# Copies of the normalised FFN input, and the split activations of the down-projection, at low SBUF offsets

## Chip, core and metric

The kernel runs on one core of one Trainium2 chip. The metric is the device time of one execution, in microseconds. Five engines work side by side and meet by semaphores: TensorE (PE; its weight loads are listed apart as PEld), VectorE (DVE), ScalarE (ACT), GpSimd (POOL) and SyncE (SP), which here only issues DMAs. SBUF is the on-chip memory that the engines read operands from: 128 partitions, and an *offset* below is the distance in KB from the start of a partition. PSUM holds what TensorE writes.

## What is computed

One trunk layer over 1024 tokens of width 1024: two groups of recurrent heads, an out-projection, and a feed-forward network with a 3x3 convolution over a grid of 16 x 64 tokens. The change touches only the last part:

```python
def _conv_ffn(h, w_up, conv_w, w_down, rows, cols):
    u = _dwconv2d(h @ w_up, conv_w, rows, cols)
    a, b = jnp.split(u, 2, axis=-1)
    return (jax.nn.silu(a) * b) @ w_down
...
        xl = xl + g1 * (jnp.concatenate([ml_l, hg_l], axis=-1) @ w_out[l])
        xl = xl + g2 * _conv_ffn(_modulate(_rmsnorm(xl, norm2_w[l]), sh2, sc2), w_up[l], ffn_conv_w[l],
                                 w_down[l], rows, GRID_W)
...
    return _rmsnorm(xl, final_norm_w)
```

`w_up` is 1024 x 5632 and `w_down` 2816 x 1024, all in float32.

## The kernel before

**Products in three parts.** To keep float32 accuracy, each operand is split into a rounded part and the rest (`wh`, `wl` of a weight; `h2h`, `h2l` of the FFN input; `gh`, `gl` of the gated activations), and each product is made of three matmuls: high x high, high x low, low x high. One matmul is 128x128 stationary by 128x512 moving, and each has its own weight load.

**Up.** The normalised FFN input stands transposed in eight pairs of tiles, `h2h[k]` and `h2l[k]` (128 x 1024, 4 KB in a partition each). 44 column tiles `ct` of `w_up` come in pairs `ct = j` and `NF + j`, j from 0 to 21 (NF = 22). `split_weights` loads 512 KB into `wst` (three buffers) from SP, ACT rounds it to `wh`, POOL subtracts to `wl` (four buffers each, two for one `ct`). `up_half` then runs 24 matmuls for each half of the tokens: `w[:, ws]` is stationary, `x[k]` (a half of `h2h[k]` or `h2l[k]`) moves. So one `ct` is 48 matmuls and one j is 96. The first pair is made before the last norm is done (`early`). `conv2` reads the result from PSUM: one ACT scaling, and eight DVE instructions on one `ct`; then Silu on ACT and the gate product on POOL fill `Gt[j]`. For the last j the result is copied to `src` first.

**Down.** Two halves of the output columns, `dh` = 0 and 1. For each block `c` of 128 rows of `w_down` (22 of them) `down_ops` makes `wh`, `wl` and, from `Gt[c]`, `gh` (ACT) and `gl` (DVE; POOL for c < 3 of `dh` = 0). Here the activations are stationary (`x[:, ts_]`) and the weights move; 24 matmuls for one `c`, three in a row for each of the eight token tiles. `kind` says where `gh` and `gl` stand: 0 for the first block, which is prepared while the up-projection still runs; 1 for the other blocks; 2 for the last NL = 4 blocks of `dh` = 1, whose 96 matmuls run token tile by token tile at the very end so that the final norm can follow tile by tile.

**Between the halves** `evac` scales the eight results of `dh` = 0 from PSUM into `ytmp` (DVE), `acc` adds them to `ys` (DVE) and squares the sum (ACT); POOL multiplies by the norm weight.

**Order.** PE's order is the order of the code. The other engines' and SP's order is made by a scheduler. Each engine works strictly in its order; a tile's buffer is reused only when all its readers are done, and a pool that takes over the space of another waits for that one's readers.

**Offsets** (in KB, from the memory plan of the built program; all of these tiles span 128 partitions):

| Tile | Before |
|---|---|
| `wst`; `wh`, `wl` | 17 to 29; 29 to 45 |
| in-projection input `hh`, `hl`; out-projection input `mh`, `ml` | 45 to 125; 53 to 117 |
| `h2h[0..7]`, `h2l[0..7]` | 159 to 191, 191 to 223 |
| `Gt[0..21]` | 45 to 133 |
| `gh`, `gl` of kind 0 | 137 to 145 |
| `gh`, `gl` of kind 1 (two buffers each) | 187 to 203 |
| `wd` and `gd` (weights and activations of kind 2) | 45 to 61, and 61 to 93 |

Of the kernel before, what the change touches and what calls it, by code (L numbers as in the profile page):

```python
# [9 lines left out]
F32 = mybir.dt.float32  # L10
F32R = mybir.dt.float32r
# [6 lines left out]
P = 128  # L18
D = 1024
KD = D // P  # L20
T = 1024
# [3 lines left out]
NLT = T // P  # L25
# [5 lines left out]
NF = DFF // P  # L31
# [38 lines left out]
SLOT = (4, 6, 8)  # L70
WARM = 4
NL = 4


@with_exitstack
def kernel(ctx: ExitStack, tc: tile.TileContext, A: dict, out: bass.AP):
# [3 lines left out]
    V, S, G, PE, SY = nc.vector, nc.scalar, nc.gpsimd, nc.tensor, nc.sync  # L80

    def pool(name, bufs=1, space=None, side=None):
        kw = {}
        if space is not None:
            kw["space"] = space
        if side is not None:
            kw["side"] = side
        return tc.tile_pool(name=name, bufs=bufs, **kw)
# [7 lines left out]
    def raw(ap):  # L96
        return ap.bitcast(F32)
# [24 lines left out]
    gd = dp.tile([P, P], F32, name="gd")  # L122
# [13 lines left out]
            halves.append((wh, wl))  # L136
        return halves

    # ------------------------------------------------------------ in-projection input h
    hp_cm = pool("h", side="left")  # L140
    hp = hp_cm.__enter__()
    hh = [hp.tile([P, TA], F32R, name=f"hh{k}") for k in range(KD)]
# [349 lines left out]
    act_cm.__enter__()  # L492
    st_cm.close()

    # ------------------------------------------------------------ in-projection
    CMO = {"mq": 0, "mk": 4, "mo": 8, "hq": 12, "zf": 16, "zb": 20, "hg": 24}

    def two(pl):
# [133 lines left out]
        V.tensor_tensor(lb, lbl[:, :, 0, :], lbm, op=ALU.mult)  # L632
        V.tensor_scalar(lbm, lb, -1.0, 1.0, op0=ALU.mult, op1=ALU.add)

    # ------------------------------------------------------------ mLSTM heads
    with ExitStack() as es:
        ml = es.enter_context(pool("ml", side="left"))
        mlw = es.enter_context(pool("mlw", bufs=2, side="left"))
# [5 lines left out]

        pass

        # gates
        tasks = []
        acc = [0.0, 0.0]

# [344 lines left out]
                cur = nx  # L995

    vp_cm.__exit__(None, None, None)
    # ------------------------------------------------------------ HGRN heads
    sgp_cm = pool("sg", bufs=3, side="right")
    sgp = sgp_cm.__enter__()  # L1000
    with ExitStack() as es:
# [254 lines left out]
            if h < H - 1:  # L1256
                hs = hg_out(h, QQ, At, SS)

        # -------------------------------------------------------- out-projection, norm2
        opp_cm, opp = lefts[0]  # L1260
        mh, mlo = {}, {}

# [77 lines left out]
    h2_cm = pool("h2", side="right")  # L1340
    h2p = h2_cm.__enter__()
    h2h = [h2p.tile([P, T], F32R, name=f"h2h{k}") for k in range(KD)]
    h2l = [h2p.tile([P, T], F32R, name=f"h2l{k}") for k in range(KD)]
    with ExitStack() as es:
# [75 lines left out]
                    next(norms, None)  # L1420
            xn = out_x1(accs)

        # -------------------------------------------------------- conv FFN: up
        def up_half(pl, halves, g):
            gs = slice(g * 512, (g + 1) * 512)
            for k in range(KD):
# [28 lines left out]
        return pl_tile(name) if i % 4 < 2 else psb.tile([P, T], F32, name=name, tag="plb")  # L1455


    Gp = ctx.enter_context(pool("G", side="left"))
    Gt = [Gp.tile([P, T], F32, name=f"G{j}") for j in range(NF)]
    g2bc = Gp.tile([P, D], F32, name="g2bc")  # L1460
    with ExitStack() as es:
        fp = es.enter_context(pool("ff", bufs=2, side="left"))
# [29 lines left out]

        pst = {}

        def down_ops(c, dh, kind):
            if c % 2 == 0:
                st = wp.tile([P, 2, 512], F32, name="wst", bufs=3)
                SY.dma_start(out=st, in_=A["wdown"][dh, c // 2].rearrange("p (a b) -> p a b", a=2))
                pst["s"] = st
                if kind == 2:  # L1500
                    pst["w"] = [Gp.tile([P, 2, 512], F32R, name="wd", tag=f"G{c - NF + NL + i}") for i in range(2)]
            src = pst["s"][:, c % 2, :]
            if kind == 2:
                wh, wl = [w[:, c % 2, :] for w in pst["w"]]
                gh, gl = [Gp.tile([P, T], F32R, name="gd", tag=f"G{NL + 2 * (c - NF + NL) + i}") for i in range(2)]
            else:
                wh = wp.tile([P, 512], F32R, name="wh", bufs=4)
                wl = wp.tile([P, 512], F32R, name="wl", bufs=4)
                gp_ = dn_ if kind else Gp
                gh = gp_.tile([P, T], F32R, name="gh")  # L1510
                gl = gp_.tile([P, T], F32R, name="gl")
            S.copy(wh, src)  # L1512
            G.tensor_tensor(wl, src, raw(wh), op=ALU.subtract)  # L1513
            S.copy(gh, Gt[c])  # L1514
            (G if dh == 0 and c < 3 else V).tensor_tensor(gl, Gt[c], raw(gh), op=ALU.subtract)  # L1515
            return gh, gl, wh, wl
# [7 lines left out]
            return src  # L1524

        for j in range(NF):
            if j == NF - 1:
                pre0 = down_ops(0, 0, 0)
            pl = up_src(j, j == NF - 1)
            conv2(Gt[j], pl, lambda i: fcw[:, j, i:i + 1])  # L1530
            S.activation(Gt[j], Gt[j], AF.Silu)
            pl = up_src(NF + j, j == NF - 1)
            cb = fp.tile([P, T], F32, name="cb", tag="cb")
            conv2(cb, pl, lambda i: fcw[:, NF + j, i:i + 1])
            G.tensor_tensor(Gt[j], Gt[j], cb, op=ALU.mult)
    h2_cm.__exit__(None, None, None)

    # ------------------------------------------------------------ conv FFN: down, final norm
    dn_ = ctx.enter_context(pool("dn", bufs=2, side="right"))
    d1 = ctx.enter_context(pool("d1", bufs=1, side="right"))  # L1540
    fnw = d1.tile([P, D], F32, name="fnw")
    SY.dma_start(out=fnw, in_=A["fnw"].partition_broadcast(P))
    ms_cm = tc.manual_schedule(engines={mybir.EngineType.PE})
    ms_cm.__enter__()
    ys = [d1.tile([P, D], F32, name=f"y{t}") for t in range(NLT)]
    s0 = d1.tile([P, NLT, 2], F32, name="s0")
    pre = [pre0]
    for dh in range(2):
# [19 lines left out]
                mm(t, c, *ops)  # L1568
        rest = [part(c, True) for c in range(n, NF)]

        def evac(t):
            tmp = dn_.tile([P, 512], F32, name="ytmp", bufs=8)
            V.tensor_tensor(tmp, po[t], g2bc[:, ds_], op=ALU.mult)
            return tmp

# [7 lines left out]
        if dh == 0:  # L1583
# [3 lines left out]
            for t, tmp in zip(order, tmps):  # L1587
                y = acc(t, tmp)
# [107 lines left out]
```

## Time and profile before

| | us |
|---|---|
| three runs | 1602.72, 1602.76, 1604.93; median 1602.76 |
| span of the profiled execution, first to last instruction (no other time of it is given) | 1603.1 |
| up-projection on PE | 833 to 1332 |
| down-projection, `dh` = 0, then `dh` = 1 | 1332 to 1464, to 1595 |
| last norm and stores | to 1603.1 |
| busy: PE, DVE, ACT, POOL | 1520.5, 1137.0, 551.4, 638.8 |

A matmul's row gives its start and a modelled end: matmuls overlap, so the duration (0.39 us) is longer than the distance from one start to the next. That distance, called the *step* below, is what a matmul costs in a dense row of them, and it is read from start times. In a merged row (x96) it is the row's length without one duration, over the count less one.

### The profile page before, as it was taken

What the parts mean: (1) busy time and instruction counts of PE and PEld (TensorE: products, weight loads), DVE (VectorE), ACT (ScalarE), POOL (GpSimd) and SP (SyncE); (2) the same over time, 40 slices, a digit from 0 to 9 for tenths busy, and PEclk for the clock granted to TensorE, in tenths of its full rate; (3) what the DMA queues carried; (4) which work ended last, traced back from release to release, by engine and by line L of the source; (5) the groups of instructions that cost most, each with busy time, mean ns of one, the idle gap of its engine ahead of it and who ended that gap; (6) DMA issues with size and microseconds to landing.
All of it is one profiled execution on the core that took longest, in us unless ns stands there. A gap on an engine that the chain in (4) does not pass through costs nothing.

```text
span 1603.1 us, 22297 instructions
## 1 busy us (share of the span) xinstructions
PE 1520.5 (95%) x8822; PEld 1223.5 (76%) x8822; DVE 1137.0 (71%) x1474; ACT 551.4 (34%) x948; POOL 638.8 (40%) x525
## 2 busy tenths in 40 slices
PE   7788899999899999999999999999999998998998
PEld 4666788888777777777867888888888886886886
DVE  7996666878577776766587888888888887226334
ACT  5542242444133342434464222222222222223332
POOL 3674234463335645433322423333233335335341
PEclk8889999999999999999999999999999999999999
DMA  9234440222032111125561111111111111411102
GB/s 371 80 126 156 161 131 28 66 67 66 27 108 67 44 52 41 40 80 173 182 217 51 45 48 53 40 53 40 53 52 41 53 37 54 158 41 40 48 31 105
DMA packets 45486, 133.37 MB, mean 83 GB/s; under 512 B 4547, under 2 KB 14659, under 8 KB 45382
## 3 DMA queue, kind: packets, MB, share of 16 engines
q1 hardware_dynamic: 45382, 131.95, 24.4%
q8 instruction: 69, 1.13, 0.3%
q14 instruction: 35, 0.29, 0.1%
HBM read 119.81 MB, written 12.13 MB: 82 GB/s over the span
## 4 chain that ended last, share of the span: by engine, by line
PE 70%; DVE 7%; POOL 3%; ACT 3%; issue 2%; DMA 1%; POOLq 0%; SPq 0%; ACTq 0%; DVEq 0%
PE pu L1430 30%; PE pd L1559 13%; PE po L1286 3%; PE pl_hg L510 3%; PE pl_zb L510 3%; PE pl_zf L510 3%; PE pl_mo L510 2%; PE pl_mq L510 2%; PE pc L510 1%; PE pl_hq L510 1%; PE ap L1089 1%; DVE G L1489 1%; POOL QQ L1126 1%; PE st L877 1%; PE pl_mk L510 1%
## 5 line engine op out<-in xcount | busy, mean ns | idle before, releaser
L135 POOL TENSOR_TENSOR wl<-wst,wh 128x512 fp32r<-128x512 f32 x114 | 150.9, 1326 | 374.9 <-ACT wh L133 361.8
L133 ACT CAST wh<-wst 128x512 fp32r<-128x512 f32 x184 | 111.9, 620 | 540.5 <-issue 226.3
L1430 PE MATMUL pu<-h2l,wh 128*128 128x512 f32 x704 | 279.0, 396 | 1.2 <-DVE h2l L1397 1.2
L1430 PE MATMUL pu<-h2h,wh 128*128 128x512 f32 x704 | 278.6, 396 | 1.5 <-ACT wh L133 1.5
L1430 PE MATMUL pu<-h2h,wl 128*128 128x512 f32 x704 | 278.5, 396 | 0.0
L1489 DVE SCALAR_TENSOR_TENSOR G<-pu,fcw,G 128x945 f32<-128x945 f32 (+2 forms) x168 | 205.2, 1222 | 30.0 <-ACT G L1482 25.1
L1489 DVE SCALAR_TENSOR_TENSOR cb<-pu,fcw,cb 128x945 f32<-128x945 f32 (+2 forms) x168 | 205.3, 1222 | 28.8 <-ACT cb L1482 23.8
L1430 PEld LDWEIGHTS pu<-h2l,wh 128*128 128x128 f32 x704 | 132.2, 188 | 35.3 <-DVE h2l L1397 3.5
L1430 PEld LDWEIGHTS pu<-h2h,wh 128*128 128x128 f32 x704 | 132.2, 188 | 33.6 <-ACT h2h L1393 1.7
L1430 PEld LDWEIGHTS pu<-h2h,wl 128*128 128x128 f32 x704 | 132.2, 188 | 31.6
L1515 DVE TENSOR_TENSOR gl<-G,gh 128x1024 fp32r<-128x1024 f32 x37 | 48.1, 1302 | 136.2 <-ACT gh L1514 136.2
L1126 POOL TENSOR_TENSOR QQ<-QQ,FF 128x256 f32<-128x256 f32 x112 | 108.4, 989 | 81.0 <-PE ap L1089 37.7
L1559 PE MATMUL pd<-wh,gl 128*128 128x512 f32 x320 | 129.6, 405 | 6.2 <-DVE gl L1515 5.3
L1559 PE MATMUL pd<-wh,gh 128*128 128x512 f32 x320 | 127.8, 400 | 4.4 <-ACT gh L1514 4.4
L1559 PE MATMUL pd<-wl,gh 128*128 128x512 f32 x320 | 128.6, 402 | 0.0
L1513 POOL TENSOR_TENSOR wl<-wst,wh 128x512 fp32r<-128x512 f32 x40 | 72.4, 1811 | 121.5 <-ACT wh L1512 121.5
L135 DVE TENSOR_TENSOR wl<-wst,wh 128x512 fp32r<-128x512 f32 x70 | 57.7, 844 | 56.9 <-ACT wh L133 56.7
L1514 ACT CAST gh<-G 128x1024 fp32r<-128x1024 f32 x40 | 41.9, 1047 | 136.9 <-PE pd L1559 132.4
L1559 PEld LDWEIGHTS pd<-wh,gl 128*128 128x128 f32 x320 | 61.4, 192 | 22.0 <-DVE gl L1515 6.2
L1559 PEld LDWEIGHTS pd<-wh,gh 128*128 128x128 f32 x320 | 61.5, 192 | 19.8 <-ACT gh L1514 4.9
L1559 PEld LDWEIGHTS pd<-wl,gh 128*128 128x128 f32 x320 | 61.4, 192 | 15.4
L329 POOL TENSOR_TENSOR wl<-wst,wh 128x512 fp32r<-128x512 f32 x26 | 50.1, 1949 | 43.9 <-ACT wh L327 24.0
(387 smaller groups left out, 3128.9 us busy)
## 6 DMA issues: line engine op xcount, KB each, us to landing
wst<-in_wup_dram SPq DMA_DIRECT2D x44, 512.0 KB, 3.2
wst<-in_wcm_dram SPq DMA_DIRECT2D x28, 512.0 KB, 3.4
wst<-in_wmod_dram SPq DMA_DIRECT2D x26, 512.0 KB, 3.4
wst<-in_wout_dram SPq DMA_DIRECT2D x24, 512.0 KB, 3.5
wst<-in_wdown_dram SPq DMA_DIRECT2D x22, 512.0 KB, 3.3
wst<-in_wvml_dram SPq DMA_DIRECT2D x10, 512.0 KB, 3.5
x<-in_xcT_dram SPq DMA_DIRECT2D x8, 512.0 KB, 6.0
wsc<-in_wsc_dram SPq DMA_DIRECT2D x8, 512.0 KB, 8.8
```

The source lines that it names most:

```text
L133: S.copy(wh, st[:, hs_])
L135: (eng or G).tensor_tensor(wl, st[:, hs_], raw(wh), op=ALU.subtract)
L329: eng.tensor_tensor(wl, si, raw(wh), op=ALU.subtract)
L510: PE.matmul(o, w[:, ws], x[k][:, c0:c1], start=(k == 0 and pi == 0), stop=(k == KD - 1 and pi == 2))
L1126: G.tensor_tensor(qv, qv, tq, op=ALU.mult)
L1286: PE.matmul(po[g], x[k][:, ts_], halves[g][wi], start=(k == 0 and pi == 0), stop=(k == KD - 1 and pi == 2))
L1430: PE.matmul(pl[:, gs], w[:, ws], x[k][:, gs], start=(k == 0 and pi == 0), stop=(k == KD - 1 and pi == 2))
L1489: V.scalar_tensor_tensor(a3[:, r0:r1, c0:c1], s3[:, r0 + dy:r1 + dy, c0 + dx:c1 + dx], wcol((dy + 1) * 3 + dx + 1), a3[:, r0:r1, c0:c1], o ...
L1513: G.tensor_tensor(wl, src, raw(wh), op=ALU.subtract)
L1514: S.copy(gh, Gt[c])
L1515: (G if dh == 0 and c < 3 else V).tensor_tensor(gl, Gt[c], raw(gh), op=ALU.subtract)
L1559: PE.matmul(po[t], x[:, ts_], w, start=(c == 0 and pi == 0), stop=(c == NF - 1 and pi == 2))
```

## The change

Three things. First, after the norm, 16 DMAs from SP copy `h2h` and `h2l` to new tiles `low` at offsets 45 to 109, eight at j = 0 and eight at j = 1 (`MOVE`); from j = 3 on, `up_half` reads the copies, and the space of the originals goes to a new pool `Gr` at the right (upper) end. Second, the tiles that held the copies then serve the down-projection: `gh`, `gl` of kind 1 take L0 to L3 (45, 49, 77 and 81), `ys` takes L4 to L11 and `ytmp` L12 to L15, two halves in one tile. Third, to make room, `Gt` is split: `Gt[0..8]` at 109 to 145, `Gt[9..21]` in `Gr` at 163 to 215. With them move `gh`, `gl` of kind 0 (215 and 219), `wd` (109 to 125) and the eight `gd` of kind 2 (125 to 145 for five, 163 to 175 for three). `wst`, `wh` and `wl` stay. No matmul, and no instruction on another engine but the 16 DMAs, is added or removed.

```diff
+NGL = 9
+MOVE = ((0, 1, 2, 3), (4, 5, 6, 7))
...
+    lo = ctx.enter_context(pool("lo", side="left"))
+    low = [[lo.tile([P, T], F32R, name=f"low{i}", tag=f"L{i}") for i in range(q, 2 * KD, 2)] for q in range(2)]
     Gp = ctx.enter_context(pool("G", side="left"))
-    Gt = [Gp.tile([P, T], F32, name=f"G{j}") for j in range(NF)]
+    Gt = [Gp.tile([P, T], F32, name=f"G{j}") for j in range(NGL)]
...
+        def g_pool(j):
+            return Gp if j < NGL else Gr
...
-                    pst["w"] = [Gp.tile([P, 2, 512], F32R, name="wd", tag=f"G{c - NF + NL + i}") for i in range(2)]
+                    pst["w"] = [g_pool(c - NF + NL + i).tile([P, 2, 512], F32R, name="wd", tag=f"G{c - NF + NL + i}")
+                                for i in range(2)]
...
-                gh, gl = [Gp.tile([P, T], F32R, name="gd", tag=f"G{NL + 2 * (c - NF + NL) + i}") for i in range(2)]
+                gh, gl = [g_pool(j).tile([P, T], F32R, name="gd", tag=f"G{j}")
+                          for j in range(NL + 2 * (c - NF + NL), NL + 2 * (c - NF + NL) + 2)]
...
-                gp_ = dn_ if kind else Gp
-                gh = gp_.tile([P, T], F32R, name="gh")
-                gl = gp_.tile([P, T], F32R, name="gl")
+                if kind:
+                    gh, gl = [lo.tile([P, T], F32R, name="gd", tag=f"L{2 * (c % 2) + i}") for i in range(2)]
+                else:
+                    gh = Gr.tile([P, T], F32R, name="gh")
+                    gl = Gr.tile([P, T], F32R, name="gl")
...
         for j in range(NF):
+            if j < len(MOVE):
+                for k in MOVE[j]:
+                    SY.dma_start(out=raw(low[0][k]), in_=raw(h2h[k]))
+                    SY.dma_start(out=raw(low[1][k]), in_=raw(h2l[k]))
+            if j == len(MOVE) + 1:
+                h2h[:], h2l[:] = low
+                h2_cm.__exit__(None, None, None)
+                Gr = ctx.enter_context(pool("Gr", side="right"))
+                Gt.extend(Gr.tile([P, T], F32, name=f"G{i}") for i in range(NGL, NF))
...
-    h2_cm.__exit__(None, None, None)
...
-    ys = [d1.tile([P, D], F32, name=f"y{t}") for t in range(NLT)]
+    ys = [lo.tile([P, D], F32, name=f"y{t}", tag=f"L{4 + t}") for t in range(NLT)]
...
+        yt = []
+        slots = itertools.cycle(range(12, 16))
+
         def evac(t):
-            tmp = dn_.tile([P, 512], F32, name="ytmp", bufs=8)
+            if not yt:
+                pair = lo.tile([P, T], F32, name="ytmp", tag=f"L{next(slots)}")
+                yt.extend((pair[:, 0:512], pair[:, 512:1024]))
+            tmp = yt.pop(0)
```

**SP's queue at the start of the up-projection.** Before, the convolution weights `fcw` are followed at once by the loads of `w_up`:

```order
L128 DMA wst_8140<-in_wup_dram 128x1024
L1367 DMA x1d6_86<-x1_7745 128x1024
L1367 DMA x1d7_87<-x1_7747 128x1024
L1467 DMA fcw_7978<-in_ffcw_dram 128x396
L128 DMA wst_8209<-in_wup_dram 128x1024
```

Now (the middle of the sixteen copies is left out):

```order
L1540 DMA low0_7938<-h2h0_7151 128x1024
L1541 DMA low1_7946<-h2l0_7159 128x1024
L1540 DMA low2_7939<-h2h1_7152 128x1024
L1541 DMA low3_7947<-h2l1_7160 128x1024
L1540 DMA low4_7940<-h2h2_7153 128x1024
L1471 DMA fcw_7984<-in_ffcw_dram 128x396
L1541 DMA low5_7948<-h2l2_7161 128x1024
```

Five copies now stand ahead of `fcw`, and all sixteen ahead of the sixth load of `w_up` (the tile `ct` = 24, second of j = 2).

**ACT at the end of the up-projection.** Here `src` is the last j's result, and the row behind `gh` or `gd` names the block (`G1` is c = 1). Before:

```order
L1523 COPY src_10850<-pu_10801 128x1024
L1482 ACTIVATE G21_7959<-src_10850,fcw_7978 128x1024
L1512 CAST wh_11018<-wst_11016 128x512
L1512 CAST wh_11050<-wst_11016 128x512
L1523 COPY src_10921<-pu_10872 128x1024
L1514 CAST gh_10986<-G1_7939 128x1024
L1531 ACTIVATE G21_7959<-G21_7959 128x1024
L1482 ACTIVATE cb_10923<-src_10921,fcw_7978 128x1024
L1514 CAST gh_11020<-G2_7940 128x1024
```

Now:

```order
L1534 COPY src_10889<-pu_10840 128x1024
L1486 ACTIVATE G21_8317<-src_10889,fcw_7984 128x1024
L1525 CAST gd_11058<-G2_7959 128x1024
L1525 CAST gd_11024<-G1_7958 128x1024
L1523 CAST wh_11056<-wst_11054 128x512
L1523 CAST wh_11088<-wst_11054 128x512
L1534 COPY src_10960<-pu_10911 128x1024
L1551 ACTIVATE G21_8317<-G21_8317 128x1024
L1486 ACTIVATE cb_10962<-src_10960,fcw_7984 128x1024
```

The rounded activations of c = 1 and 2 have moved ahead of the weights of those blocks; their tiles are free once `low0` to `low3` have been read for the last time.

**POOL at the same place.** Before:

```order
L1535 TENSOR_TENSOR G20_7958<-G20_7958,cb_10770 128x1024
L1513 TENSOR_TENSOR wl_11019<-wst_11016,wh_11018 128x512
L1513 TENSOR_TENSOR wl_11051<-wst_11016,wh_11050 128x512
L1515 TENSOR_TENSOR gl_10987<-G1_7939,gh_10986 128x1024
L1515 TENSOR_TENSOR gl_11021<-G2_7940,gh_11020 128x1024
```

Now:

```order
L1555 TENSOR_TENSOR G20_8316<-G20_8316,cb_10809 128x1024
L1526 TENSOR_TENSOR gd_11059<-G2_7959,gd_11058 128x1024
L1526 TENSOR_TENSOR gd_11025<-G1_7958,gd_11024 128x1024
L1524 TENSOR_TENSOR wl_11057<-wst_11054,wh_11056 128x512
L1524 TENSOR_TENSOR wl_11089<-wst_11054,wh_11088 128x512
```

The two subtractions for the activations have moved ahead of the two for the weights, and c = 2 ahead of c = 1. DVE's order differs only in how the two convolutions of the first j are interleaved.

## Rows read from the trace of the kernel before

**Rows 1.** The page: busy time of each engine, and the 40 slices.

```profile
PE 1520.5 (95%) x8822; PEld 1223.5 (76%) x8822; DVE 1137.0 (71%) x1474; ACT 551.4 (34%) x948; POOL 638.8 (40%) x525
...
GB/s 371 80 126 156 161 131 28 66 67 66 27 108 67 44 52 41 40 80 173 182 217 51 45 48 53 40 53 40 53 52 41 53 37 54 158 41 40 48 31 105
```

**Rows 2.** Stretches: busy PE, PEld, DVE, ACT, POOL (instructions), PEclk, DMA share, GB/s.

```profile
862.00:1321.00 459.00, 459.00 (x1972) 369.73 (x1972) 404.13 (x333) 114.00 (x145) 155.03 (x102) 1.00 0.14 46
1332.30:1337.90 5.60, 5.60 (x26) 4.61 (x25) 5.49 (x4) 2.41 (x3) 4.97 (x2) 1.00 0.28 94
1355.00:1361.00 6.00, 5.82 (x14) 4.58 (x15) 2.37 (x3) 0.00 (x0) 4.52 (x2) 0.50 0.06 13
1361.00:1458.00 97.00, 97.00 (x417) 78.03 (x416) 20.82 (x17) 26.66 (x34) 30.79 (x17) 1.00 0.27 94
1573.00:1594.00 21.00, 21.00 (x94) 17.33 (x93) 13.03 (x20) 8.68 (x18) 5.62 (x18) 1.00 0.30 123
```

**Rows 3.** Time order, PE, up-projection: j = 3 starts, last tile starts.

```profile
906.61 0.40 PE L1430 MATMUL pu<-h2h,wh 128*128 128x512 f32 x1
...
1321.01 0.40 PE L1430 MATMUL pu<-h2h,wh 128*128 128x512 f32 x1
```

**Rows 4.** Time order, PE, down-projection: inside c = 0, inside c = 1.

```profile
1333.37 0.39 PE L1559 MATMUL pd<-wh,gl 128*128 128x512 f32 x1
...
1337.45 0.40 PE L1559 MATMUL pd<-wh,gl 128*128 128x512 f32 x1
...
1338.72 0.40 PE L1559 MATMUL pd<-wl,gh 128*128 128x512 f32 x1
...
1343.39 0.39 PE L1559 MATMUL pd<-wh,gh 128*128 128x512 f32 x1
```

**Rows 5.** Time order, PE: the last 96 matmuls, merged.

```profile
1573.27 21.96 PE L1559 MATMUL pd<-wd,gd 128*128 128x512 f32 x96
```

**Rows 6.** The end of up: time order of PE, DVE and ACT.

```profile
1350.42 0.40 PE L1559 MATMUL pd<-wl,gh 128*128 128x512 f32 x1
1355.18 0.80 PE L1559 MATMUL pd<-wh,gl 128*128 128x512 f32 x1 [4.36 <-DVE gl L1515]
...
1323.79 15.30 DVE L1489 SCALAR_TENSOR_TENSOR G<-src,fcw,G 128x1008 f32<-128x1008 f32 x8 [2.21 <-ACT G L1482]
1341.37 12.62 DVE L1489 SCALAR_TENSOR_TENSOR cb<-src,fcw,cb 128x1008 f32<-128x1008 f32 x7 [2.28 <-ACT cb L1482]
1353.91 1.22 DVE L1515 TENSOR_TENSOR gl<-G,gh 128x1024 fp32r<-128x1024 f32 x1
```

**Rows 7.** Between the halves: time order of DVE, ACT and PE.

```profile
1458.21 1.05 ACT L1514 CAST gh<-G 128x1024 fp32r<-128x1024 f32 x1 [4.03 <-PE pd L1559]
...
1460.43 4.90 DVE L1573 TENSOR_TENSOR ytmp<-pd,g2bc 128x512 f32<-128x512 f32 x8
...
1478.57 1.03 ACT L1514 CAST gh<-G 128x1024 fp32r<-128x1024 f32 x1
...
1474.81 0.40 PE L1559 MATMUL pd<-wh,gl 128*128 128x512 f32 x1
1479.65 0.50 PE L1559 MATMUL pd<-wh,gh 128*128 128x512 f32 x1 [4.45 <-ACT gh L1514]
```

**Rows 8.** The start of up: time order of DVE, SP, ACT and PE.

```profile
846.09 0.42 DVE L1397 TENSOR_TENSOR h2l<-ntmp,h2h 128x256 fp32r<-128x256 f32 x1
...
853.77 0.33 SPq L1467 DMA_DIRECT2D fcw<-in_ffcw_dram  x1
...
881.42 0.62 ACT L133 CAST wh<-wst 128x512 fp32r<-128x512 f32 x1 [0.46 <-PE pu L1430]
...
895.41 0.40 PE L1430 MATMUL pu<-h2h,wh 128*128 128x512 f32 x1
```

**Rows 9.** DMA issues: engine, count, KB each, median us to landing.

```profile
wst<-in_wup_dram SPq DMA_DIRECT2D x44, 512.0 KB, 3.2
```

## The prediction

> **What bounds the kernel now.** I read the page first: PE is busy for 95% of the span, DVE for 71%, and ACT and POOL for less than half [rows 1]. From the stretches, the up-projection shows PE busy for all of 862 to 1321, at a granted clock of 1.00, which is the level of 2.4 GHz, while DVE works 404 of 459 us [rows 2]. So in the feed-forward part, time is the number of matmuls times the step from one start to the next, plus two places where PE waits. The change removes no matmul; it can only act through the step or through the waits. So the view that decides is the one that is easily passed over: start times in time order, set against where the operands stand.
>
> In the up-projection, j = 3 starts at 906.61 and the last tile, `ct` = 43, at 1321.01 [rows 3]. Between them lie 37 tiles of 48 matmuls: 414.40 / 1776 = 233.3 ns a step. Here the weights (stationary) stand at 29 to 45 KB and the input (moving) at 159 to 223.
>
> In the down-projection, the matmuls inside c = 0 go from 1333.37 to 1337.45 in 18 steps, 226.7 ns each; those inside c = 1, from 1338.72 to 1343.39, in 20 steps of 233.5 [rows 4]. Same line, same shape, same weights' buffers, five microseconds apart, at the same granted clock (1.00 over c = 0 and again from 1361 on) [rows 2]. What differs is that the stationary operand of c = 0 stands at 137 to 145 KB, and that of c = 1 at 187 to 203. The last 96 matmuls, with weights at 45 to 61 and activations at 61 to 93, take (21.96 - 0.39) / 95 = 227.1 [rows 5].
>
> So there are two steps: 233.3 where one of the two operands stands at 159 KB or above, 226.7 to 227.1 where both stand below 150. It is not the neighbours' work: during c = 0, DVE is busy for 5.49 of 5.60 us and POOL for 4.97, much more than in 1361 to 1458 (DVE 20.82 of 97 us), where 417 matmuls, those that straddle its ends among them, started at the slow step [rows 2]. The difference is 6.2 to 6.6 ns a matmul; I take 6.6, since the 18 steps of c = 0 lie in the same kind of loop, and keep 6.2 as the lower end.
>
> **The change part by part.**
>
> *Up-projection.* From j = 3 the moving operand stands at 45 to 109, the weights at 29 to 45: both low. Of the tiles that read the copies, the 37 from 906.61 to 1321.01 [rows 3] count on the path: 1776 x 6.6 = 11.7 us (11.0 at 6.2). The 48 matmuls of `ct` = 43 get faster too, but that is given back (below). The next bound is DVE: it works 404 us in 459, or 88% [rows 2]; with the stretch 2.8% shorter that is 91%, so it does not take over. POOL and ACT are far from it.
>
> *Down-projection, kind 1.* `gh`, `gl` go from 187 to 203 down to 45 to 85. What counts is bounded by the two waits. At the end of up, PE waits at c = 3 of `dh` = 0, until 1355.18, for DVE: after the last `src` for G, DVE does eight instructions (15.30 us), waits 2.28 for ACT, does seven more (12.62), then `gl` [rows 6]. That chain starts when PE has finished the tile before `ct` = 43, at 1321.01, and ends 34.2 us later whatever PE does meanwhile. So all that PE wins in `ct` = 43, c = 1 and c = 2 (72 + 24 matmuls, about 0.6 us) only makes the wait longer, and what c = 0 loses by going up to 215 (0.16 us) makes it shorter. Between the halves a chain likewise runs from the end of c = 20 (ACT's cast at 1458.21) through eight `ytmp` (4.90 us), the additions and ACT's cast at 1478.57 to PE's restart at 1479.65 [rows 7]; c = 21 and the first two blocks of `dh` = 1 win nothing. What counts is c = 3 to 20 of `dh` = 0 and c = 2 to 17 of `dh` = 1: 34 blocks x 24 = 816 matmuls. About 13 after each wait run at the granted clock of 0.50 (1.2 GHz) [rows 2] and I count nothing for them: 790 x 6.6 = 5.2 us (4.9 at 6.2).
>
> *Kind 2 and the tail.* Of the last 12 matmuls for a token tile, the 3 of c = 21 and the 1 that reads `gl` of c = 20 get stationary operands at 163 to 175: 32 of 96, at most 32 x 6.6 = 0.2 us lost, at least nothing, since no row shows an operand between 163 and 187 as stationary. I take the loss, the nearest rows (159 and 187) being slow: -0.2.
>
> *The sixteen copies.* 16 x 512 KB = 8.4 MB on the DMA queue from SP, none hidden by an idle PE: their cover is the time until someone waits. They can start when the first pair is written, at 846.5 (the DVE row at 846.09 ends it) [rows 8]. Behind them on SP stands the load of `ct` = 24. ACT casts that tile at 881.42, and PE starts it at 895.41 [rows 8]; cast and subtraction need about 2 us for its first half, so the load may land as late as 893 before PE waits. That leaves 46 us, of which the load itself takes 3.2 [rows 9]: 43 us for the copies, 195 GB/s. The trace has no copy from SBUF to SBUF, so I bound it: the first slice of 40 us moved 371 GB/s [rows 1], giving 23 us; one transfer at a time at 3.2 us each [rows 9] gives 51 us and 8 us of waiting. I take the first, since sixteen DMAs queued together are like that slice, not like single loads: no cost. The copies themselves are needed at 906.61, later still. Five of them stand ahead of `fcw`, issued at 853.77 [rows 8]; at 371 GB/s those five take 7 us from 846.5 and are done by then.
>
> The Trainium skill ("SBUF — State Buffer", section "Summary: rules for kernel authors") gives 436 GB/s between SBUF and SBUF; as an estimate from that figure the copies would take 19 us, and the sum stays the same.
>
> *Moved steps.* At the end of up, ACT and POOL now make `gh`, `gl` of c = 2 and 1 before the weights of c = 1. POOL's longer queue (two subtractions more ahead of `wl` of c = 1) may make PE wait at c = 1 for up to 2 us, and this too falls into the slack of the DVE chain above; no cost. If that cover is gone, it costs those 2 us.
>
> *Sum.* 11.7 + 5.2 - 0.2 = 16.7 us from the profiled span of 1603.1: 1586.4. That span is 0.3 above the median of the runs, 1602.76, so the forecast is 1602.8 - 16.7 = **1586 us**.
>
> **The rivals.**
>
> *One side alone.* What slows the step may be only the moving operand's place, or only the stationary's, in the sense that one of the two stages has another cause. For it: the two stages differ in which operand is high. Against: each is slow, and c = 0 and the last 96 show the fast step where both are low. Up alone: 1602.8 - 11.7 = 1591; down alone: 1602.8 - 5.0 = 1598.
>
> *The step does not follow the place*, but something in c = 0 and the last 96 that I did not see. Then PE keeps 233.3 and all else is hidden: 1603, no change. For it: 24 and 96 matmuls are few. Against: the two stretches have nothing else in common.
> The Trainium skill ("TensorE: Matmul & The Clock Gate", section "Back-to-back issue gap") would lead there: it has the gap depend on the columns and the clock alone, 512 / 2.4 + 2.5 = 216 ns as an estimate, wherever the operands stand. The trace does not bear it out: at one granted clock and one shape it shows 226.7 and 233.5 [rows 4].
>
> *The copies crawl.* A copy between two places of one memory reads and writes the same ports; if it goes at 105 GB/s, 16 of them take 80 us, `ct` = 24 lands 80 - 43 = 37 us late, PE stands still and the gain of 17 is lost: 1602.8 - 16.7 + 37 = 1623, slower than before. It costs from 195 GB/s down and decides from 140 (60 us). For it: no row shows such a copy. Against: HBM loads of the same 4 KB rows went at 371 GB/s [rows 1].
>
> **How the numbers follow.** Full gain with the waits as they are, 1583 to 1589.5: 0.72. One side alone, or copies that cost some microseconds, 1589.5 to 1599: 0.12. Better than 1583, if a wait gets shorter: 0.04. No change: 0.08. Slower: 0.04. The likeliest gives 1586. Below it, the range takes in a gain of 2 us in the two waits and half a step's uncertainty, from 1582; above it, the lower end of the step difference (1587), POOL's 2 us, the 8 us of one-at-a-time copies or the up side alone: to 1594. A measurement of this kernel can tell about 0.2% (3.2 us) from no change; faster by more than that takes the first three cases, 0.88; within it 0.08; slower 0.04.
>
> **What would show it.** In the changed kernel's trace, the start of j = 3 to the start of `ct` = 43 should take 1776 x 226.7 = 402.6 us and not 414.4; j = 0 to 2 should stay at 233.3 a step. Blocks c = 3 to 20 should go from 5.60 us each to 5.44; c = 0 from 5.44 to 5.60. PE's wait at c = 3 should grow from 4.4 to between 5 and 6 us, ending 34 us after the start of `ct` = 43. Nobody should wait for `low`, and ACT's cast of `ct` = 24 should still follow PE, not the DMA. I am wrong if the step in j = 3 and later reads 233, or if PE shows a gap before 907 that a DMA ended.

## The result, and the profile after

The changed kernel takes **1585.46 us** (1585.19 to 1587.04) against 1602.74 (1601.0 to 1604.93): a ratio of 0.9902, with a 95% interval from 0.9887 to 0.9918. The forecast was 1586. The profiled execution has a span of 1583.4 us, 19.7 less than before. Of that, 2.6 us lie ahead of the up-projection, which starts at 830.42 instead of 833.00; the change touches nothing there, and another kernel below whose edit lies behind this point (the even blocks moved back up) starts up at 828.42, so this is taken as a difference between executions. From the start of up to the end of the span it is 770.1 us before and 753.0 after: **17.1 us gained**, where the sum said 16.7. (The prediction set the span of 1603.1 beside the median of the times, but a span is 1.8 us shorter than the time of the same execution, as in 1583.4 and 1585.19. The profiled execution of the kernel before was thus the longest of its runs, 1604.93; the forecast does not hang on this.)

The page, busy time and the 40 slices, answering [rows 1]. PE is busy for 15.6 us less:

```profile
PE 1504.9 (95%) x8822; PEld 1226.3 (77%) x8822; DVE 1136.1 (72%) x1474; ACT 551.2 (35%) x948; POOL 639.1 (40%) x525
...
GB/s 368 88 121 158 171 121 40 67 57 72 32 108 70 42 55 42 30 74 140 218 205 284 54 41 54 53 41 53 52 42 54 43 38 159 54 54 41 43 38 106
```

The changed kernel's stretches, columns as in [rows 2]: up, c = 0, the restart after the wait at c = 3, and the blocks behind it:

```profile
862.00:1306.60 444.60, 444.60 (x1957) 367.25 (x1956) 401.18 (x331) 113.34 (x144) 154.86 (x102) 1.00 0.16 54
1317.40:1323.00 5.60, 5.60 (x26) 4.50 (x25) 5.53 (x3) 1.54 (x2) 5.60 (x3) 1.00 0.40 151
1340.80:1347.00 6.20, 6.20 (x15) 4.92 (x16) 2.18 (x2) 0.00 (x0) 4.52 (x2) 0.52 0.11 42
1347.00:1445.00 98.00, 98.00 (x434) 81.10 (x434) 23.64 (x21) 28.26 (x36) 32.62 (x18) 1.00 0.15 52
```

The stretch of up has 1957 matmuls in 444.6 us, where 1972 took 459.0 before; DVE works 90% of it (88% before), and the granted clock is 1.00 as before. In down, 434 matmuls start within 98 us, where 417 did within 97.

Time order on PE: j = 3 starts, `ct` = 43 starts (as [rows 3]); the wait at c = 3 (as [rows 6]); the restart between the halves (as [rows 7]); the last 96 matmuls (as [rows 5]):

```profile
904.02 0.63 PE L1432 MATMUL pu<-low,wh 128*128 128x512 f32 x2
...
1306.61 0.61 PE L1432 MATMUL pu<-low,wh 128*128 128x512 f32 x2
...
1334.19 0.39 PE L1578 MATMUL pd<-wl,gd 128*128 128x512 f32 x1
1340.79 1.22 PE L1578 MATMUL pd<-wh,gd 128*128 128x512 f32 x2 [6.20 <-DVE gd L1526]
...
1457.23 0.39 PE L1578 MATMUL pd<-wh,gd 128*128 128x512 f32 x1
1462.50 0.61 PE L1578 MATMUL pd<-wh,gd 128*128 128x512 f32 x1 [4.89 <-ACT gd L1525]
...
1553.43 22.14 PE L1578 MATMUL pd<-wd,gd 128*128 128x512 f32 x96
```

The up stretch takes 1306.61 - 904.02 = 402.6 us, 226.7 ns a step, as forecast. The tiles of j = 0 to 2 still read `h2h` and `h2l`, and those of them that wait for nothing keep 11.2 us. The wait at c = 3 grew from 4.36 to 6.20 us and ends 34.2 us after 1306.61: the same distance as before, so it took back what PE had won in the blocks ahead of it. The last 96 lost 0.18 us.

The copies on SP's queue, and ACT's first cast of `ct` = 24 (as [rows 8]):

```profile
842.92 0.53 SPq L1540 DMA_DIRECT2D low<-h2h  x1
...
851.17 0.34 SPq L1471 DMA_DIRECT2D fcw<-in_ffcw_dram  x1
...
862.66 1.48 SPq L1541 DMA_DIRECT2D low<-h2l  x1
864.24 19.75 SPq L130 DMA_DIRECT2D wst<-in_wup_dram  x4
...
878.83 0.62 ACT L135 CAST wh<-wst 128x512 fp32r<-128x512 f32 x1 [4.38 <-issue]
```

All sixteen are issued within 21.3 us; the first cast of `ct` = 24 stands where it stood before (878.83 against 881.42, 2.6 us earlier like the whole stage), and PE waits nowhere for `low`.

### The profile page after: what moved, and what is told of

Read it like the earlier page. It is cut to its first block, busy times and chain, and to the rows that moved or that the text cites. A ratio compares the mean times of both kernels' runs of the same rounds, so it can differ in the third digit from the quotient of the medians.

```text
span 1583.4 us, 22327 instructions
## 1 busy us (share of the span) xinstructions
PE 1504.9 (95%) x8822; PEld 1226.3 (77%) x8822; DVE 1136.1 (72%) x1474; ACT 551.2 (35%) x948; POOL 639.1 (40%) x525
## 4 chain that ended last, share of the span: by engine, by line
PE 71%; DVE 7%; POOL 2%; issue 2%; ACT 2%; DMA 1%; POOLq 0%; SPq 0%; ACTq 0%; DVEq 0%
PE pu L1432 29%; PE pd L1578 14%; PE po L1288 3%; PE pl_hg L512 3%; PE pl_zb L512 3%; PE pl_zf L512 3%; PE pl_mo L512 2%; PE pl_mq L512 2%; PE pc L512 1%; PE pl_hq L512 1%; PE ap L1091 1%; DVE G L1493 1%; POOL QQ L1128 1%; PE st L879 1%; PE pl_mk L512 1%
## 5 line engine op out<-in xcount | busy, mean ns | idle before, releaser
L1432 PE MATMUL pu<-low,wh 128*128 128x512 f32 x1216 | 374.5, 389 | 0.0
L135 ACT CAST wh<-wst 128x512 fp32r<-128x512 f32 x184 | 112.0, 620 | 529.6 <-issue 227.5
L1432 PEld LDWEIGHTS pu<-low,wh 128*128 128x128 f32 x1216 | 228.3, 188 | 47.4
L1432 PE MATMUL pu<-low,wl 128*128 128x512 f32 x608 | 236.5, 389 | 0.0
L1578 PE MATMUL pd<-wh,gd 128*128 128x512 f32 x624 | 196.7, 397 | 11.7 <-DVE gd L1526 6.9
L1526 DVE TENSOR_TENSOR gd<-G,gd 128x1024 fp32r<-128x1024 f32 x41 | 57.1, 1393 | 131.2 <-ACT gd L1525 131.0
L1578 PEld LDWEIGHTS pd<-wh,gd 128*128 128x128 f32 x624 | 119.6, 192 | 38.3 <-DVE gd L1526 8.0
L1432 PEld LDWEIGHTS pu<-low,wl 128*128 128x128 f32 x608 | 114.2, 188 | 23.6
L1578 PE MATMUL pd<-wl,gd 128*128 128x512 f32 x312 | 123.6, 396 | 0.0
L1578 PEld LDWEIGHTS pd<-wl,gd 128*128 128x128 f32 x312 | 59.8, 192 | 12.7
L1555 POOL TENSOR_TENSOR G<-G,cb 128x1024 f32<-128x1024 f32 x22 | 53.9, 2451 | 14.9 <-DVE cb L1493 14.9
```

The lines of the kernel that those rows point to most:

```text
L135: S.copy(wh, st[:, hs_])
L1432: PE.matmul(pl[:, gs], w[:, ws], x[k][:, gs], start=(k == 0 and pi == 0), stop=(k == KD - 1 and pi == 2))
L1578: PE.matmul(po[t], x[:, ts_], w, start=(c == 0 and pi == 0), stop=(c == NF - 1 and pi == 2))
```

## The experiments

So the time and its two main terms came out. The reason given was that the step depends on how high an operand stands. The runs below test that first.

**Does the place set the step?** A kernel that runs rows of 48 matmuls of 512 columns, with tiles of the same data at sixteen offsets from 29 to 217 KB, all of them whole KB, as moving or stationary operand:

```
    for i in range(count):
        PE.matmul(ps[:, 0:n], st[:, (i % 4) * P:(i % 4 + 1) * P], mv[:, 0:n], ...)
```

> This kernel leaves the layer out: it only runs rows of 48 dense matmuls (128x128 stationary, 128x512 moving, the same shape as in the FFN), each row with its two operands at two chosen offsets in a partition; its output means nothing. Read: the step of each row, (length - 0.39) / 47. Theory A (an operand above some border between 150 and 160 KB is slow, whichever it is): both at or below 149 KB give 226.7 ns, any row with an operand at 161 KB or above gives 233.3, and both high also gives 233.3 or more. Theory B (it is the two standing in different regions): 29 with 189 gives 233.3, but 189 with 173, 205 or 217 gives 226.7. Theory C (it grows with the distance): 29 with 125 lies between 226.7 and 233.3, and 145 with 157 is fast. Theory D (the place has nothing to do with it): all rows alike.

Time order on PE; in `pr<-o61k,o29k` the moving operand stands at 61 KB and the stationary one at 29:

```profile
18.15 11.04 PE L106 MATMUL pr<-o61k,o29k 128*128 128x512 f32 x48
...
170.47 11.04 PE L106 MATMUL pr<-o217k,o29k 128*128 128x512 f32 x48
...
344.55 11.04 PE L106 MATMUL pr<-o29k,o217k 128*128 128x512 f32 x48
...
442.47 11.04 PE L106 MATMUL pr<-o217k,o189k 128*128 128x512 f32 x48
```

Every row of 512 columns but the first (13.05 us) and the very last (11.15) takes 11.04 us, (11.04 - 0.39) / 47 = 226.6 ns a step. The place in KB does nothing. The theory behind the forecast fell here, although the kernel had gained what it said.

**Is the gain really tied to what was moved?** Two kernels take back a part of it. In the first, `gh` and `gl` of the even blocks of down go back up:

```diff
-    gh, gl = [lo.tile([P, T], F32R, name="gd", tag=f"L{2 * (c % 2) + i}") for i in range(2)]
+    gh, gl = ([lo.tile([P, T], F32R, name="gd", tag=f"L{2 + i}") for i in range(2)] if c % 2 else
+              [Gr.tile([P, T], F32R, name=n, tag=n) for n in ("gh", "gl")])
...
```

> The changed kernel, but the split activations of the even blocks c of kind 1 stand at 215 and 219 KB instead of 45 to 53; the odd ones stay low. If the place of the stationary operand sets the step: even blocks take 24 x 233.3 = 5.60 us, odd ones 5.44, within one stage and one run; of the blocks that count (c = 4 to 20 of the first half, 2 to 16 of the second) 17 are even, so 17 x 0.16 = 2.7 us longer than the changed kernel, about 1588.2. If the place does not matter: all blocks 5.44 and 1585.5.

1586.51 us (1583.63 to 1588.56), ratio 0.9911 [0.9887, 0.9934]. Time order on PE, the starts of c = 4, 5 and 6:

```profile
1346.58 0.39 PE L1579 MATMUL pd<-wh,gh 128*128 128x512 f32 x1
...
1352.17 0.39 PE L1579 MATMUL pd<-wh,gd 128*128 128x512 f32 x1
...
1357.62 0.39 PE L1579 MATMUL pd<-wh,gh 128*128 128x512 f32 x1
```

5.59 us for a block that reads `gh`, 5.45 for one that reads `gd`, in turn. These rows tell, not the time: from the start of up to the end of the span the profiled execution takes 1.9 us more than the changed kernel's (2.7 expected), but the medians differ by 1.0 us only, with runs 5 us apart. In the second kernel, the loop goes over to the copies at j = 9 instead of 3:

```diff
-            if j == len(MOVE) + 1:
+            if j == NGL:
```

> The changed kernel, but the up-projection goes over to the copies at j = 9 instead of j = 3, so 6 x 96 = 576 matmuls more read the originals. If the moving operand's place sets the step: j = 3 to 8 take 22.4 us each and j = 9 on 21.76, in all 576 x 6.67 = 3.8 us longer than the changed kernel, about 1589.3. If the gain of the up stage has another cause: 1585.5, with no jump of the step at j = 9.

1589.23 us (1585.45 to 1591.12; 1589.3 expected), ratio 0.9926 [0.9902, 0.995]. Time order on PE, the second tile of j = 8, then both tiles of j = 9:

```profile
1029.65 0.40 PE L1432 MATMUL pu<-h2h,wh 128*128 128x512 f32 x1
...
1040.85 0.62 PE L1432 MATMUL pu<-low,wh 128*128 128x512 f32 x2
...
1051.73 0.62 PE L1432 MATMUL pu<-low,wh 128*128 128x512 f32 x2
```

Tiles take 11.2 us up to j = 8 and 10.88 from j = 9. So in both kernels the step changes with the tile that an instruction reads. With the first probe, something other than the place must tell those tiles apart.

**Are the copies hidden because there is room?** Each copy made three times, all in a row:

```diff
-            if j < len(MOVE):
-                for k in MOVE[j]:
+            for k in [k for _ in range(3) for m in MOVE for k in m] if j == 0 else ():
+                if True:
...
```

> The changed kernel with each of the sixteen copies made three times (48 DMAs from SP, 25 MB), to find where their cover ends. By the prediction's account the load of the tile ct = 24 may land some 46 us after the first copy starts. In the changed kernel 16 copies were issued within 21 us; 48 then take about 64 us, the load lands at about 843 + 64 + 3 = 910, PE wants the tile at 892.8 and needs some 2 us after the landing: a wait of 19 us and a cold clock after it, so about 1606. If the cover is longer than I think (the loads have a way past the copies, or there are more tiles in hand): no change, 1585.5.

1605.86 us, ratio 1.0027 [1.0012, 1.0041]. Time order on PE, and the stretch around the wait (columns as in [rows 2]):

```profile
894.45 0.40 PE L1432 MATMUL pu<-h2h,wl 128*128 128x512 f32 x1
913.99 0.80 PE L1432 MATMUL pu<-h2h,wh 128*128 128x512 f32 x1 [19.15 <-ACT wh L135]
...
880.00:915.00 35.00, 15.85 (x66) 12.13 (x64) 24.84 (x21) 5.95 (x7) 4.53 (x3) 0.77 1.01 396
```

With 48 copies the load of `ct` = 24 lands too late by the 19 us that the account of the cover gave. After the wait, the next tile takes 14.03 us, 2.8 more than such a tile at a granted clock of 1.00. The cover was told rightly.

**Start addresses.** In the program, the tiles in the upper half stand in pools laid down from byte 229,344, which is 32 bytes short of 224 KB; those in the lower half count from a round address. So the move also changed where a tile starts within a small block of bytes. The next probe holds shifts of 0 to 112 bytes, once in tiles at 21 to 57 KB (`l`), once at 161 to 197 (`h`):

```
SH = (0, 16, 32, 48, 64, 80, 96, 112)
...
            PE.matmul(ps[:, 0:n], t[s][:, a + (i % 4) * P:a + (i % 4 + 1) * P], t[m][:, b:b + n],
```

> This kernel leaves the layer out: rows of 48 dense matmuls of the FFN's shape, each with two operands whose start is 0 to 112 bytes past a multiple of 128, around 21 to 57 KB (l) or 161 to 197 KB (h); its output means nothing. The first map of offsets, all of whose operands start at a multiple of 128, had one step of 226.6 ns from 29 to 217 KB. Theory E (the start within a line of 64 bytes): operands at 0 and 64 give 226.6, at 16, 32, 48, 80, 96 and 112 more, about 233.3 at 32 and 96, which is where the originals and the old activations stand; low and high alike. Theory G (a multiple of 128 is wanted): 64 is slow as well. Theory F (what costs is that high operands alternate with others from matmul to matmul, which no row here does): all rows 226.6.

Time order on PE, moving operand named first:

```profile
28.99 11.37 PE L109 MATMUL pr<-l32b,l0b 128*128 128x512 f32 x48
...
106.71 11.05 PE L109 MATMUL pr<-l0b,l16b 128*128 128x512 f32 x48
...
206.70 11.09 PE L109 MATMUL pr<-h32b,l32b 128*128 128x512 f32 x48
...
283.71 11.35 PE L109 MATMUL pr<-h32b,l0b 128*128 128x512 f32 x48
...
350.48 11.36 PE L109 MATMUL pr<-l0b,h16b 128*128 128x512 f32 x48
...
440.02 11.16 PE L109 MATMUL pr<-l96b,l32b 128*128 128x512 f32 x48
```

The slow step is there: 11.37 us is 233.6 ns. It comes low and high alike (13 of 14 pairs of rows agree within 0.02 us; the exception is below), and it goes when both operands are shifted by the same 32 bytes (227.7). So it isn't each operand's alignment by itself that counts, but the one start against the other.

One pair of rows does not fit this, nor any account given here: with the stationary operand alone shifted by 16 bytes the row takes 11.05 us low (`l0b,l16b`) and 11.36 high (`l0b,h16b`). What follows goes by multiples of 32 bytes.

Two kernels then hold that against the whole program. The first is the kernel *before* with 96 and 32 bytes reserved, so that the upper tiles start at multiples of 128 bytes; the second is the *changed* kernel with 32 bytes reserved ahead of the lower tiles:

```diff
+    h2p.tile([P, 24], F32, name="edge")
...
+            dn_.tile([P, 8], F32, name="edge", bufs=1)
```

```diff
+    lo.tile([P, 8], F32, name="edge")
```

> The kernel before, with no copies and no tile moved lower: 96 bytes are reserved above the FFN input's tiles and 32 above the down-projection's, so that the originals at 159.9 to 223.9 KB and the split activations at 187.9 to 203.9 KB start at multiples of 128 bytes instead of 96 and 32 past one. If the start within a line is the cause: all 44 up tiles take 48 x 226.7 = 10.88 us and every block of the down-projection 5.44; 84 + 5 tiles' worth, so from the kernel before (42 tiles from 860 on, 2016 x 6.6 = 13.3, less 0.3 given back, plus 5.2): 18.2 us less, about 1583.5, as fast as the change or 1 to 2 us faster. If it is the place (or alternation of high and low): no change, 1602, with 233.3 ns a step.

> The changed kernel with 32 bytes reserved below its copies, so that the copies and the split activations of kind 1, all still at 45 to 106 KB, start 32 bytes past a multiple of 128. If the start within a line is the cause: the gain is gone, 233.3 ns a step in both stages, 1602 or so (up to 0.6 more, since the blocks of kind 2 lose too). If low offsets are the cause: 1585.5, steps of 226.7.

The first takes 1598.77 us (1596.13 to 1603.13), ratio 0.9981 [0.9966, 0.9996]; the second 1600.95 (1596.97 to 1604.54), ratio 0.999 [0.9975, 1.0006]. The starts of j = 3 and `ct` = 43 in the second:

```profile
906.16 0.63 PE L1432 MATMUL pu<-low,wh 128*128 128x512 f32 x2
...
1320.56 0.63 PE L1432 MATMUL pu<-low,wh 128*128 128x512 f32 x2
```

414.4 us, 233.3 ns a step: the tiles are low, the copies are made, and 32 bytes take nearly all of the gain away. In the first kernel 412.7 us, 232.4 ns: round addresses alone don't bring it either, and the 1583.5 us that the expectation gave for them were missed; the weights there start at 0 modulo 256 and the tiles at 128.

**The rule of the two starts.** The same probe over both operands' shifts from 0 to 480 bytes; stationary first in the pairs:

```
SH = tuple(range(0, 512, 32))
ROWS = [(0, d) for d in SH] + [(d, 0) for d in SH] + [(d, d) for d in SH]
```

> This kernel leaves the whole layer out: it runs rows of 48 TensorE matmuls of 512 columns, and the two operands' tiles stand a chosen number of bytes past a whole KB. First the moving operand shifted by 0 to 480 bytes in steps of 32 with the weights unshifted, then the weights shifted alone, then both by the same amount, then a mixed list with rows out of order. Theory now (operands' starts relative to each other): the rows with both shifted alike stay at 226.6 to 228 ns a step for every shift, and rows with a difference that is not a multiple of 512 bytes (or of 256, which this row would tell apart) read up to 233.4 ns, the same for plus and minus where the difference modulo the period is the same. Rival (start of each operand by itself): both-alike rows are slow wherever the single-shift rows are, about 229 to 233 ns at 32, 96 and so on. Rival (history: the step depends on the row before, not on the addresses): the mixed list, which repeats differences of 0, 224, 256, 352 and 480 behind other rows, gives other steps than the ordered rows for the same pair by over 2 ns.

Time order on PE (`a32b,a0b`: moving operand 32 bytes past a whole KB, stationary at 0; one name where both stand in the same tile):

```profile
28.57 11.37 PE L105 MATMUL pr<-a32b,a0b 128*128 128x512 f32 x48
39.77 11.16 PE L105 MATMUL pr<-a64b,a0b 128*128 128x512 f32 x48
...
61.98 11.36 PE L105 MATMUL pr<-a128b,a0b 128*128 128x512 f32 x48
73.18 11.40 PE L105 MATMUL pr<-a160b,a0b 128*128 128x512 f32 x48
...
106.80 11.05 PE L105 MATMUL pr<-a256b,a0b 128*128 128x512 f32 x48
...
128.89 11.16 PE L105 MATMUL pr<-a320b,a0b 128*128 128x512 f32 x48
...
229.21 11.40 PE L105 MATMUL pr<-a0b,a96b 128*128 128x512 f32 x48
...
262.81 11.16 PE L105 MATMUL pr<-a0b,a192b 128*128 128x512 f32 x48
...
428.61 11.08 PE L105 MATMUL pr<-a160b 128*128 128x512 f32 x48
```

The step follows the difference, moving start minus stationary start, modulo **256** bytes. A difference of 0 (also 256) gives 226.8 to 227.5 ns, whatever the common shift; 64 (also 320, and -192) gives 229.2; 160 (also -96) 234.3; each other multiple of 32 gives 232.6 to 233.6. The mixed list at the end repeats the times for the same differences to within 0.04 us a row, so it isn't the row before.

The same rule put to the whole program: the kernel before with its pads chosen so that the upper tiles start at the same address modulo 512 as the weights.

```diff
+    h2p.tile([P, 56], F32, name="edge")
...
+            dn_.tile([P, 40], F32, name="edge", bufs=1)
```

> The kernel before, with no copy and nothing moved to the lower half: 224 bytes are reserved beside the FFN input's 16 tiles and 160 bytes beside the down-projection's split activations, so that in the upper half, where they stood before, both start at the same address modulo 512 bytes as the weights that they are multiplied with. Theory now (operands' starts relative to each other): up tiles of 10.88 us (226.7 ns a step) instead of 11.2 from j = 0 on, down blocks of 5.44 us instead of 5.60: 38 tiles and 6 more that the copies miss by 16 that the change wins at j = 4 and later, so 2112 x 6.6 ns = 13.9 us for up and 790 x 6.6 ns = 5.2 us for down, about 1584 us, no slower than the change. Rival (low half): no gain, 1602.7 and tiles of 11.2 us. Rival (alignment to 64 or 128 bytes only, of which a pad of another size gave tiles of 11.15 us): 1599 to 1601, blocks of 5.55 to 5.60.

1582.94 us (1580.96 to 1583.85), ratio 0.9875 [0.9847, 0.9902]: no copy, nothing moved by more than 224 bytes, and as fast as the change (the median is 2.5 us lower, but the intervals of the two ratios overlap). j = 3 and `ct` = 43:

```profile
902.69 0.39 PE L1431 MATMUL pu<-h2h,wh 128*128 128x512 f32 x1
...
1305.25 0.39 PE L1431 MATMUL pu<-h2h,wh 128*128 128x512 f32 x1
```

402.6 us, 226.7 ns, in the upper half. All programs fall in line (the differences are from the memory plans of the built programs):

| kernel | up: difference mod 256, step | down (kind 1): difference, block |
| --- | --- | --- |
| before | 224: 233.3 ns | 96: 5.60 us |
| changed | 0: 226.7 | 0: 5.44 |
| even blocks back up | 0: 226.7 | 32 and 0 in turn: 5.59, 5.45 |
| upper tiles at multiples of 128 | 128: 232.4 | 128: 5.60 |
| lower tiles shifted by 32 | 32: 233.3 | 224: 5.60 |
| same start, no copies | 0: 226.7 | 0: 5.44 |

**What else was to be had.** Two edits on top of the last kernel, aimed at the two waits: the Silu of the last j comes behind the scale copies (first alone), then also the sums of the first half of the columns are written later, among the blocks of the second half.

```diff
-            S.activation(Gt[j], Gt[j], AF.Silu)
+            if j < NF - 1:
+                S.activation(Gt[j], Gt[j], AF.Silu)
...
+            if j == NF - 1:
+                S.activation(Gt[j], Gt[j], AF.Silu)
```

> The same kernel with the first of the two edits alone: the Silu of the last j behind the scale copies. By the account above 1582.94 - 2.2 = about 1580.7 us, the gap at c = 3 (4.90 us) about 2 us shorter. Rival (the copies of the last j do not bound that chain, the multiplication on GpSimd behind them or the VectorE sums do): no change, 1582.9, the gap at c = 3 as it was.

1579.47 us (1578.7 to 1586.07), ratio 0.9869 [0.9838, 0.9899]. Time order on PE at c = 3, then the stretches behind the restart, of the kernel without this edit and with it:

```profile
1339.40 0.80 PE L1560 MATMUL pd<-wh,gl 128*128 128x512 f32 x1 [4.51 <-DVE gl L1516]
...
1339.40:1344.40 5.00, 5.00 (x13) 3.98 (x14) 2.19 (x2) 0.00 (x0) 3.86 (x2) 0.55 0.00 0
```

```profile
1338.09 0.50 PE L1563 MATMUL pd<-wh,gl 128*128 128x512 f32 x1 [3.21 <-DVE gl L1516]
...
1338.10:1343.00 4.90, 4.90 (x21) 4.04 (x22) 2.18 (x2) 0.00 (x0) 3.77 (x2) 1.00 0.00 0
```

From start to start, the gap shrank from 4.91 to 3.60 us, by 1.3, not by the 2 expected. But after it the granted clock stayed at 1.00 where it had been 0.55, and block c = 3 takes 8.99 us instead of 12.35: 2.1 us beside the wait. That makes 3.4 us where 2.2 were forecast: in these two executions the edit is worth more through the clock behind the wait than through the wait. The medians differ by 3.5 us, but one run took 1586.07 and the intervals of the two ratios overlap, so the times alone do not show it.

```diff
-            for t, tmp in zip(order, tmps):
-                y = acc(t, tmp)
-                G.tensor_tensor(y, y, fnw[:, ds_], op=ALU.mult)
+            late = [lambda t=t, tmp=tmp: add(t, tmp, ys[t][:, 0:512]) for t, tmp in zip(order, tmps)]
...
+            if dh == 1 and c >= 2 and late:
+                late.pop(0)()
```

> The kernel with both operands at the same start modulo 256 bytes and no copies (1582.94 us), with two more edits that the theory of the operands' starts says nothing of: the Silu of the last j comes on ScalarE behind the scale copies of the second convolution, and the eight sums of the first half of the output columns are spread over blocks c = 2 to 9 of the second half. In the profile of that kernel the last Silu's delay is part of the 4.90 us gap at c = 3, and the first half's sums stand ahead of the second half's first splits on VectorE, where TensorE waits 5.25 and 1.10 us. Expected by that account: about 2.2 us from the first edit and 5.25 + 1.10 - 2 x 0.23 = 5.9 us from the second, so 1574.8 us, the gap between the halves under 1 us. Rival (VectorE has no room in blocks c = 2 to 9 of the second half, so that the sums delay the splits there): waits of 0.5 to 1 us in each of those eight blocks, and 1579 to 1582 us.

1575.91 us (1574.47 to 1579.57), ratio 0.9837 [0.9815, 0.9858], the lowest median of all, 3.6 us below the former (again with overlapping intervals) and 1.1 above the forecast. Time order on DVE, then on PE, at block c = 2 of the second half, where the kernel without this edit has gaps of 5.27 and 1.10 us, and the stretches behind the two restarts, at c = 3 of the first half and here (columns as in [rows 2]):

```profile
1444.14 9.78 DVE L1594 TENSOR_TENSOR y<-y,ytmp 128x512 f32<-128x512 f32 x7
1453.84 2.28 DVE L1516 TENSOR_TENSOR gl<-G,gh 128x1024 fp32r<-128x1024 f32 x1
...
1456.18 0.78 PE L1563 MATMUL pd<-wh,gl 128*128 128x512 f32 x1 [3.23 <-DVE gl L1516]
...
1338.40:1343.30 4.90, 4.88 (x21) 4.05 (x22) 2.21 (x2) 0.00 (x0) 3.74 (x2) 1.00 0.00 0
1456.20:1461.00 4.80, 4.80 (x14) 3.83 (x15) 3.02 (x2) 2.18 (x4) 4.80 (x4) 0.64 0.00 0
```

The wait for ACT's `gh` is gone, but not the delay: DVE runs seven of the eight sums in one piece ahead of the `gl` of c = 2, since there the order on DVE is the scheduler's and not that of the text. PE's gap in that block is 3.6 us. Neither the expectation (under 1 us) nor its rival (waits in each of eight blocks) came true. The two restarts also say something of the clock: at c = 3 this kernel repeats what the former showed, a gap of 3.60 us and a granted clock of 1.00 behind it; here, behind a gap of 3.62 us, it is 0.64. So the length of the gap alone does not tell what comes behind it.

## Why the prediction was right, and where it was not

*The sizes.* Up was priced at 11.7 us; it measured 414.4 - 402.6 = 11.8. Down was priced at 5.2 less 0.2 for kind 2; from the restart at c = 3 to the end of the last matmul PE took 240.05 us before and 234.77 after, 5.3 us less. Up's tiles ahead of j = 3 gave nothing, as said. Sum 17.1 against 16.7.

*The waits.* That they are ends of DVE's and ACT's chains, and take back what PE wins ahead of them, was right to the tenth at c = 3: 34.2 us from `ct` = 43 to the restart, before and after. The gap between the halves grew from 4.84 to 5.27 us, from start to start. The up to 2 us of POOL at c = 1 did not show: that block takes 5.44 us.

*The copies.* Hidden, as taken. Three times as many cost 19 us of waiting by the same account, so that the rival in which they crawl is answered by a number: the queue issued one copy of 512 KB every 1.29 us there, about 406 GB/s, more than the 371 that the prediction counted with.

*The step that failed* is the sentence "So there are two steps: 233.3 where one of the two operands stands at 159 KB or above, 226.7 to 227.1 where both stand below 150." The rows under it are right, the reading is not. In the kernel before, c = 0 and the last 96 matmuls [rows 4, 5] are those stretches of down where both operands start at the same address modulo 256, and the others [rows 3, 4] differ by 224 and by 96. Being low and starting alike fell together, since the upper pools are laid down from an address 32 bytes short of a round one, and the prediction looked at addresses in KB only. The move removed the difference by the way. That the number came true, to half a microsecond, was luck as far as the cause goes, and the run of the change could not have told: the place would have given the same numbers in every row named as a sign.

*The rival that was half right.* "The step does not follow the place" was true. It went on to "then PE keeps 233.3", which does not follow: the hidden cause can change along with the place. Against it the prediction said that "the two stretches have nothing else in common"; that was a claim about what had been looked at. The Trainium skill ("TensorE: Matmul & The Clock Gate", section "Back-to-back issue gap") gives a formula in which the gap depends on columns and clock alone, but gives it for an isolated matmul; of a stream with weight loads, which is what runs here, it says that both operations set the spacing, and the prediction left that out. The trace does not agree with the formula: at one shape and at a granted clock of 1.00 the step goes from 226.7 to 233.3 ns with the operands' starts.

*Kind 2* lost what was forecast (22.14 - 21.96 = 0.18 us), again for the other reason: the third of its matmuls that lost reads stationary operands whose start differs from the weights' by 32 bytes.

What stays open: why the difference counts, why 64 costs less than its neighbours, and the two rows with a shift of 16 bytes that disagree. No run here looks inside.

## What to carry to other kernels

Where two stretches of equal matmuls differ by a few per cent at one granted clock, list the start address of both operands in bytes, and not only in KB: in this kernel a few hundred bytes of padding did all that the move of 16 tiles did. Before a forecast from two kinds of stretches is believed, a probe should vary one property alone; a change that moves something alters several. And a wait that shortens may be worth more than its length, where the granted clock no longer falls behind it; which gap does that was not found here.

## What the runs showed of the hardware that was not expected

- The step of fp32r matmuls of 512 columns is 226.6 ns at best and up to 234.3 ns, by the moving operand's start less the stationary one's, modulo 256 bytes, for starts at multiples of 32 bytes; at equal starts 29 to 217 KB make no difference.
- Shifts of 16 bytes have their own values: both operands at 16 or 48 read 11.21 us for 48 matmuls (230.2 ns), both at 32 or 64 11.09; the stationary one alone at 16 reads 11.05 in a low tile and 11.36 in a high one.
- Directly behind rows of 128 columns, a row of 512 columns took a little longer: 11.15 us where the same pair of tiles had taken 11.04 in the first probe, 11.22 against 11.16 in the second. The next rows there took what they had taken before (11.07 against 11.09, 11.37 twice). The cause is not known.
- SBUF-to-SBUF copies of 512 KB, queued together, kept all DMA engines busy: 396 GB/s over 35 us (with the first loads behind the copies), beside a PE that kept its tiles of 11.2 us until the wait.
